# Gate stage of an expert mixer: four PSUM banks for gate matmuls, two for turns, index copies issued by GpSimd, 58 early blocks

## The chip, the cores and the metric

The kernel runs on one core of a Trainium2 chip. A core has five engines, each with its own queue of instructions: TensorE (PE, matmuls), VectorE (DVE), ScalarE (ACT), GpSimd (POOL) and SyncE (SP, which here only issues DMAs). On-chip data lies in SBUF; matmuls write into PSUM, which has eight banks of 128 x 512 32-bit words. The metric is the device time of one launch in microseconds (us), lower is better.

## The reference, cut to what matters

Two layers, each a token mixer (a gated convolution in layer 0, a scan in layer 1) followed by PEER, a mixer over single-neuron experts. The change lies in PEER, which runs for 640 tokens (512 latent, 128 context) of width 1024:

```python
def peer(h, wq, keys, u, v):
    q = (t @ wq).reshape(T, PEER_HEADS, 2, PEER_KEY_DIM // 2)
    s = jnp.einsum('thpe,hpne->thpn', q, keys).astype(jnp.float32)
    s1, i1 = lax.top_k(s[:, :, 0], PEER_TOPK)
    s2, i2 = lax.top_k(s[:, :, 1], PEER_TOPK)
    cand = (s1[..., :, None] + s2[..., None, :]).reshape(T, PEER_HEADS, PEER_TOPK * PEER_TOPK)
    cidx = (i1[..., :, None] * N_KEYS + i2[..., None, :]).reshape(T, PEER_HEADS, PEER_TOPK * PEER_TOPK)
    sc, pos = lax.top_k(cand, PEER_TOPK)
    idx = jnp.take_along_axis(cidx, pos, axis=-1)
    g = jax.nn.softmax(sc, axis=-1).astype(h.dtype)
    ...
        act = jnp.einsum('td,thkd->thk', tb, u[ib])
        return jnp.einsum('thk,thkd->td', jax.nn.gelu(act, approximate=False) * gb, v[ib])
```

There are 128 x 128 = 16384 experts, and each token takes 16 for each of 8 heads, 128 (expert, gate) pairs in all.

## The kernel before, in words

For 464 of the tokens PEER is computed densely: every expert's activation for every token, times a gate that is zero for most. For the other 176 tokens (16, 32 and 128, three groups) the rows of the experts that they chose are gathered from memory.

The experts are cut into 128 blocks of 128. For each there is a U block (activations: 8 pieces of the width, three matmuls each of 128 x 464, since every operand is split into a high and a low part; 24 matmuls into the PSUM tile `pact`, then a gelu by ScalarE into an SBUF tile `ga`, L511) and a V block (`rot` and `acc`, also in threes). A U weight tile of 512 KB is loaded by SP (`ur`, L84), rounded by ScalarE (`uh`, L92), and VectorE takes the rest (`ul`, L101). `mm3` (L128 to L130) issues the three matmuls.

`peer_gates` first computes the queries, top-k lists, expert numbers and gates. Then it copies the expert numbers (`last`) and gates (`SC`) of the first two gathered groups into the columns `cidx` and `cgate`, 24 small DMAs per layer (L935; 8 pairs of 16 x 16 words, 4 pairs of 32 x 32). Then comes the gate stage, which makes the dense gates of the 464 tokens: three times four transposes turn the two parts of the expert numbers and the gates (`gT`, L953, sources I1, I2, SC), each followed by a copy by ScalarE (L956, L958); then 29 chunks of 16 tokens, each with four one-hot tiles by VectorE, four groups of eight matmuls into the PSUM tile `pg` (L999, L1000), each followed by a ScalarE copy into `st` (L1001), and every two chunks a store of `st` to memory (`gdram`). The last four chunks stand in the order of the code; before them a scheduler sets the order of the instructions of each engine.

All through `peer_gates`, `fill` puts in U matmuls to keep PE busy. The U blocks that are done this way (the first `NSP`) are called early blocks; their `ga` is stored to memory by GpSimd (`adram`, L513) and loaded again by SP in the main loop (`load_act`, L570). `ga` has a ring of `LAG + 2` = 5 buffers. The PSUM budget is two banks for `pact`, one for `gT` and three for `pg`.

Then `peer` goes on in the order of the code. It starts two gathers of expert rows (L592) and the load of the first gate tile `gt` (L564) on GpSimd's queue, runs the early blocks that are left but for the last, loads the first three stored blocks, makes `h = ga * gt` for two blocks (L577 on VectorE, rounding `h1` on ScalarE), runs the last early block, and enters the loop over V blocks. An iteration loads and splits a V tile, loads the stored block three ahead (or computes U block a + 3, once the early ones are used up), makes an h, and runs 24 V matmuls: two banks' worth go through `rot`, which VectorE copies or adds into `sacc` (L647, L649). `GATHER` says how many gathered rows are begun per iteration on average while early blocks are used and after.

Of the kernel before, what the change touches and what calls it, by code (L numbers as in the profile page):

```python
# [9 lines left out]
F32 = mybir.dt.float32  # L10
# [11 lines left out]
P = 128  # L22
NL = 512
# [4 lines left out]
G0 = (0, NX[0], sum(NX))  # L28
# [3 lines left out]
HALF = 320  # L32
EPS = 1e-6
NBLK = 128
NSP = 56
LAG = 3
GA = 4
TB = 16
# [1 line left out]
SW = 64  # L40
CH = 5
FILL_Q = (0, 8500)
GATHER = (0.60, 1.98)
START = 4
MORE = (1, 1, 0, 4)
ADA_C = 16
# [70 lines left out]
class K:  # L117
# [28 lines left out]
    def run(s):  # L146
        nc, A = s.nc, s.A
        with ExitStack() as ctx:
# [4 lines left out]
            s.gdram = dram.tile([NBLK // GA, P, ND // SG, GA, SG], F32, name="gdram")  # L153
            s.adram = dram.tile([NSP, P, ND], F32, name="adram")
            s.sdram = dram.tile([1, 2, D], F32, name="sdram")
# [328 lines left out]
    def peer(s, i):  # L484
        nc, A = s.nc, s.A
        with ExitStack() as ctx:
# [15 lines left out]
            def u_blocks():  # L502
                for a in range(NBLK):
# [7 lines left out]
                    nc.scalar.activation(g, pa, AF.Gelu)  # L511
                    if a < NSP:
                        nc.gpsimd.dma_start(s.adram[a], g)  # L513
# [7 lines left out]
            def fill(ns, steps=0):  # L521

                state["owe"] += ns
                while (steps > 0 or ns and state["owe"] > 0) and state["n"] < NSP * KT:
                    t = next(ub)
                    if not steps:
                        state["owe"] -= t
                    steps -= 1 if steps else 0
                    state["n"] += 1
                U.split(state["n"] // KT + 2)  # L530
# [8 lines left out]
            with ExitStack() as mc:  # L539
# [27 lines left out]
                def load_act(a):  # L567
                    if a < NSP:
                        t = ring.tile([P, ND], F32, name="ga")
                        nc.sync.dma_start(t, s.adram[a])  # L570
                        ga[a] = t
# [60 lines left out]
                state["owe"] = 0  # L632
                fill(0, NSP * KT - state["n"] - KT)
                for a in range(LAG):
# [16 lines left out]
                for a in range(NBLK - 2):  # L651
                    V.high(a + 2)
                    if a + LAG >= NSP:
                        U.high(a + LAG + 2)
# [21 lines left out]

                    credit += GATHER[0] if a + LAG < NSP else GATHER[1]
                    due, before = 0, slot
# [72 lines left out]
    def peer_gates(s, i, hi, lo, hrow, cidx, cgate, wq, fill, V, order):  # L751
        nc, A = s.nc, s.A
        with ExitStack() as pc:
# [41 lines left out]
            with qx:  # L795
# [91 lines left out]
                for m in range(16):  # L887

                    o = s.proj_now(wq.get(m), hi, lo, qps, "pq", (lambda: fill(0, 1)) if m == 0 else None, m == 0)
# [31 lines left out]
                def fl(t, n):  # L921
                    return t[:, n].rearrange("p h k -> p (h k)")
# [8 lines left out]
                for g, m in enumerate(NX):  # L931
                    p0 = P - NL + ND + G0[g]
                    for n in range(P // m):
                        for dst, src in ((cidx, last), (cgate, fl(SC, 3))):
                            nc.sync.dma_start(dst[n * m:(n + 1) * m, G0[g]:G0[g] + m], src[p0:p0 + m, n * m:(n + 1) * m])  # L935

            with ExitStack() as gx:
                op = s.pool(gx, "oh", bufs=2)
                sp = s.pool(gx, "stage", bufs=2)
                gps = s.pool(gx, "gps", space=PSUM)  # L940
                tt = s.pool(gx, "tt")

                rep = tt.tile([P, P], F16, name="rep")
                nc.gpsimd.iota(rep, pattern=[[1, P]], base=0, channel_multiplier=0,
                               allow_small_or_imprecise_dtypes=True)
                T1 = tt.tile([P, ND, 2], F16, name="T1")
                T2 = tt.tile([P, ND, 2], F16, name="T2")
                gh = tt.tile([P, ND, 2], F16, name="gh")
                gl = tt.tile([P, ND, 2], F16, name="gl")
                for n, src in ((0, I1), (1, I2), (2, SC)):  # L950
                    o = gps.tile([P, NL], F32, name="gT", bufs=1)
                    for t in range(4):
                        nc.tensor.transpose(o[:, t * P:(t + 1) * P], fl(src, t), s.ident)  # L953
                    twice = o[:, :ND, None].to_broadcast([P, ND, 2])
                    if n < 2:
                        nc.scalar.activation((T1, T2)[n], twice, AF.Copy)  # L956
                    else:
                        nc.scalar.activation(gh, twice, AF.Copy, scale=4096.0)  # L958
                        nc.vector.scalar_tensor_tensor(gl, twice, 4096.0, gh, op0=ALU.mult, op1=ALU.subtract)
                V.prime()  # L960
                TB4 = [P, TB, P // 2, 2]
                OH = {}

                def one_hots(c):
                    sl = slice(c * TB, (c + 1) * TB)
                    pairs = rep.rearrange("p (e b) -> p e b", b=2)[:, None].to_broadcast(TB4)

                    def b(v):
                        return v[:, sl, None, :].to_broadcast(TB4)

                    def new(name, **kw):
                        t = op.tile([P, TB, P], F16, name=name, **kw)
                        return t, t.rearrange("p t (e b) -> p t e b", b=2)

                    _, o2 = new("o2", bufs=1)
                    nc.vector.tensor_tensor(o2, b(T2), pairs, op=ALU.is_equal)
                    o1, o = new("o1")
                    nc.vector.tensor_tensor(o, b(T1), pairs, op=ALU.is_equal)
                    oh, o = new("oh")
                    nc.vector.tensor_tensor(o, b(gh), o2, op=ALU.mult)  # L980
                    ol, o = new("ol")
                    nc.vector.tensor_tensor(o, b(gl), o2, op=ALU.mult)
                    OH[c] = o1, oh, ol

                fill(FILL_T)
                one_hots(0)
                for c in range(ND // TB):
                    if c == ND // TB - G_LAST:
                        order.enter_context(s.tc.manual_schedule())
                    if (c + 1) * TB < ND:  # L990
                        one_hots(c + 1)
                    fill(FILL_G if c < ND // TB - G_LAST else FILL_L)
                    o1, oh, ol = OH.pop(c)
                    if c % 2 == 0:
                        st = sp.tile([P, NBLK // GA, 2, GA, SG], F32, name="st")
                    for t in range(0, TB, 4):
                        g = gps.tile([P, 4, P], F32, name="pg", bufs=3)
                        for q in range(4):
                            nc.tensor.matmul(g[:, q, :], oh[:, t + q, :], o1[:, t + q, :], start=True, stop=False)  # L999
                            nc.tensor.matmul(g[:, q, :], ol[:, t + q, :], o1[:, t + q, :], start=False, stop=True)  # L1000
                        nc.scalar.activation(st[:, :, c % 2, :, t:t + 4], g.rearrange("p t (b a) -> p b a t", a=GA),  # L1001
                                             AF.Copy, scale=1.0 / 4096.0)
                    if c % 2 or c == ND // TB - 1:
                        n = c % 2 + 1
                        nc.scalar.dma_start(
                            s.gdram[:, :, c + 1 - n:c + 1].rearrange("g p c a t -> p g (c a t)"),
                            st[:, :, :n].rearrange("p g c a t -> p g (c a t)"))
# [464 lines left out]
```

## Time and profile before

| | us |
|---|---|
| median of three runs | 4063.26 |
| the three runs | 4061.71, 4071.17, 4063.26 |
| profiled execution | 4057.71 |
| its span in the trace | 4056.0 |
| PE busy | 3915.4 |
| VectorE busy | 3394.0 |
| ScalarE busy | 1663.2 |
| GpSimd busy | 514.9 |

The profiled execution is one more run, with a recording; the numbers of the rows below are of it. Busy times of engines lie beside each other. An engine can be idle because it waits for another; the trace names the releaser. PE's clock can be below full speed ("PEclk" 1.00), and then a busy PE does less.

### The profile page before, as it was taken

The page shows a single profiled execution, that of the slowest core. Times are in us where ns is not written, and L with a number is a line of the kernel's source. Part 1 is how long each engine was busy: PE and PEld are TensorE (multiplying, and loading weights), DVE is VectorE, ACT ScalarE, POOL GpSimd, SP SyncE. Part 2 cuts the span into 40 slices and gives each one's busy share as a digit, 9 for nine tenths or more (in the row PEclk, how much of TensorE's full clock was granted, in tenths as well). Part 3 has the DMA queues.
Part 4 walks back from the last instruction along what each step waited for, and adds up shares of the span by engine and source line. Part 5 has one row for each costly group of instructions (what it writes and reads, how often), then busy time and mean ns, then how long its engine had stood idle before and what let it go on. Part 6 is the DMA issues. An engine that isn't in the chain of part 4 may idle for free.

```text
span 4056.0 us, 59421 instructions
## 1 busy us (share of the span) xinstructions
PE 3915.4 (97%) x22237; PEld 3548.9 (87%) x22237; DVE 3394.0 (84%) x6512; ACT 1663.2 (41%) x3120; POOL 514.9 (13%) x695
## 2 busy tenths in 40 slices
PE   8999999899999999999999999999989999999998
PEld 6989988788888888888899998998878888888887
DVE  8978988588878888887999856998768888888887
ACT  5233344433334333336555644334433333343333
POOL 0010000011112212211110101000011111121211
PEclk9999999999999999999999999999999999999999
DMA  6643258988889989973333234226888898998995
GB/s 228 218 154 121 83 171 248 287 318 312 329 311 338 341 325 333 339 274 126 114 102 119 88 114 173 83 99 192 251 296 314 316 334 316 337 335 329 333 333 222
DMA packets 337451, 979.15 MB, mean 241 GB/s; under 512 B 39371, under 2 KB 174795, under 8 KB 291081
## 3 DMA queue, kind: packets, MB, share of 16 engines
q1 hardware_dynamic: 146922, 508.73, 35.7%
q0 software_dynamic: 64000, 398.47, 26.4%
q10 hardware_dynamic: 126240, 68.16, 5.9%
q8 instruction: 174, 2.85, 0.3%
q14 instruction: 115, 0.94, 0.1%
HBM read 867.00 MB, written 108.14 MB: 240 GB/s over the span
## 4 chain that ended last, share of the span: by engine, by line
issue 41%; PE 29%; DVE 15%; POOL 9%; DMA 4%; ACT 2%; POOLq 0%; SPq 0%; ACTq 0%; DVEq 0%
POOL uv L592 9%; PE pact L128 2%; DMA ur<-uT 2%; PE pact L130 2%; PE pj L128 2%; PE pact L129 2%; PE pj L129 2%; PE pj L130 2%; DVE ul L101 2%; DVE wl L101 1%; PE bank L128 1%; PE bank L129 1%; PE bank L130 1%; PE bank L1189 1%; PE pg L999 1%
## 5 line engine op out<-in xcount | busy, mean ns | idle before, releaser
L128 PE MATMUL pact<-hnh,uh 128*128 128x464 f32 x2048 | 774.2, 378 | 1.0 <-DVE xt L623 1.0
L130 PE MATMUL pact<-hnh,ul 128*128 128x464 f32 x2048 | 768.3, 375 | 0.0
L129 PE MATMUL pact<-hnl,uh 128*128 128x464 f32 x2048 | 766.6, 374 | 0.0
L592 POOL DMA_INDIRECT uv<-uv,cidx x352 | 362.2, 1029 | 1698.6 <-DVE cacc L609 1567.2
L128 PE MATMUL acc<-h,wh 128*128 128x464 f32 x1536 | 575.4, 375 | 0.0
L130 PE MATMUL acc<-h,wl 128*128 128x464 f32 x1536 | 575.3, 375 | 0.0
L129 PE MATMUL acc<-h,wh 128*128 128x464 f32 x1536 | 573.1, 373 | 0.0
L92 ACT ACTIVATE wh<-wr 128x1024 fp32r<-128x1024 f32 x385 | 404.9, 1052 | 377.8 <-DMA wr<-uv 92.5
L599 DVE SCALAR_TENSOR_TENSOR uv<-uv,hrow 128x1024 f32<-128x1024 f32 x352 | 430.1, 1222 | 128.5 <-DMA uv<-uv,cidx 125.3
L101 DVE TENSOR_TENSOR wl<-wr,wh 128x1024 fp32r<-128x1024 f32 x385 | 469.8, 1220 | 54.7 <-ACT wh L92 54.4
L609 DVE SCALAR_TENSOR_TENSOR cacc<-uv,dg,cacc 128x1024 f32<-128x1024 f32 x346 | 443.4, 1282 | 0.0
L130 PEld LDWEIGHTS pact<-hnh,ul 128*128 128x128 f32 x2048 | 386.4, 189 | 45.5 <-DVE ul L101 0.3
L128 PEld LDWEIGHTS pact<-hnh,uh 128*128 128x128 f32 x2048 | 387.2, 189 | 44.6 <-DVE xt L623 1.3
L129 PEld LDWEIGHTS pact<-hnl,uh 128*128 128x128 f32 x2048 | 387.2, 189 | 44.3
L511 ACT ACTIVATE ga<-pact 128x464 f32<-128x464 f32 x256 | 141.8, 554 | 582.6 <-PE pact L130 578.9
L101 DVE TENSOR_TENSOR ul<-ur,uh 128x1024 fp32r<-128x1024 f32 x256 | 312.1, 1220 | 56.0 <-ACT uh L92 55.9
L92 ACT ACTIVATE uh<-ur 128x1024 fp32r<-128x1024 f32 x256 | 268.3, 1050 | 184.7 <-PE pact L129 81.0
L129 PEld LDWEIGHTS acc<-h,wh 128*128 128x128 f32 x1536 | 291.0, 189 | 36.0
L130 PEld LDWEIGHTS acc<-h,wl 128*128 128x128 f32 x1536 | 290.0, 189 | 34.9
L128 PEld LDWEIGHTS acc<-h,wh 128*128 128x128 f32 x1536 | 290.7, 189 | 33.8
L601 ACT ACTIVATE dg<-dg 128x1 f32<-128x1 f32 x352 | 70.6, 200 | 540.4 <-DVE uv L599 540.0
L586 DVE TENSOR_TENSOR h<-h,h 128x464 fp32r<-128x464 f32 x256 | 163.8, 640 | 127.7 <-PE rot L129 123.8
(346 smaller groups left out, 7978.1 us busy)
## 6 DMA issues: line engine op xcount, KB each, us to landing
ur<-uT SPq DMA_DIRECT2D x256, 512.0 KB
wr<-uv SPq DMA_DIRECT2D x256, 512.0 KB
gt<-gdram SPq DMA_DIRECT2D x62, 928.0 KB
gdram<-st ACTq DMA_DIRECT2D x28, 2048.0 KB
mw<-ada_wT SPq DMA_DIRECT2D x80, 512.0 KB
adram<-ga POOLq DMA_DIRECT2D x112, 232.0 KB, 4.1
ga<-adram SPq DMA_DIRECT2D x112, 232.0 KB
wr<-ssd_w SPq DMA_DIRECT2D x48, 512.0 KB
```

Source lines behind the costliest of these rows:

```text
L92: s.K.nc.scalar.activation(hi.rearrange("p a b -> p (a b)"), s.raw[s.nh], AF.Copy)
L101: s.K.nc.vector.tensor_sub(lo.rearrange("p a b -> p (a b)"), s.raw.pop(s.ns), hi.rearrange("p a b -> p (a b)").bitcast(F32))
L128: mm(out, wh, mh, start=start, stop=False)
L129: mm(out, wh, ml, start=False, stop=False)
L130: mm(out, wl, mh, start=False, stop=stop)
L511: nc.scalar.activation(g, pa, AF.Gelu)
L586: nc.vector.tensor_sub(h2, h, h1.bitcast(F32))
L592: nc.gpsimd.indirect_dma_start(out=t[:], out_offset=None, in_=A["uv"].rearrange("l e d -> (l e) d"), in_offset=bass.IndirectOffsetOnAxis(a ...
L599: nc.vector.scalar_tensor_tensor(UV[n][:, :D], UV[n][:, :D], 1.0, rows[-1], op0=ALU.mult, op1=ALU.mult, accum_out=dg[:, n:n + 1])
L601: nc.scalar.activation(dg[:, n:n + 1], dg[:, n:n + 1], AF.Gelu)
L609: nc.vector.scalar_tensor_tensor(cacc, t[:, D:], dg[:, n:n + 1], cacc, op0=ALU.mult, op1=ALU.add)
L999: nc.tensor.matmul(g[:, q, :], oh[:, t + q, :], o1[:, t + q, :], start=True, stop=False)
```

## The change

`NSP` goes from 56 to 58, so two more U blocks of each layer are computed before the loop and reloaded in it. `gT` gets a second PSUM bank and `pg` a fourth, so the gate stage uses all eight banks. The 24 small copies of L935 are issued by GpSimd instead of SP. `GATHER` is a little higher.

```diff
-NSP = 56
+NSP = 58
...
-GATHER = (0.60, 1.98)
+GATHER = (0.62, 2.0)
...
                         for dst, src in ((cidx, last), (cgate, fl(SC, 3))):
-                            nc.sync.dma_start(dst[n * m:(n + 1) * m, G0[g]:G0[g] + m], src[p0:p0 + m, n * m:(n + 1) * m])
+                            nc.gpsimd.dma_start(dst[n * m:(n + 1) * m, G0[g]:G0[g] + m], src[p0:p0 + m, n * m:(n + 1) * m])
...
                 for n, src in ((0, I1), (1, I2), (2, SC)):
-                    o = gps.tile([P, NL], F32, name="gT", bufs=1)
+                    o = gps.tile([P, NL], F32, name="gT", bufs=2)
...
                     for t in range(0, TB, 4):
-                        g = gps.tile([P, 4, P], F32, name="pg", bufs=3)
+                        g = gps.tile([P, 4, P], F32, name="pg", bufs=4)
```

The order of the instructions on PE at the first two turns of layer 0 (`gT` is the bank, `I_2740` and `I_2741` the two sources; `pact` rows are U matmuls), before:

```order
L953 MATMUL gT<-ident,I_2740 128x128 x4
L128 MATMUL pact<-hnh,uh 128x464
L129 MATMUL pact<-hnl,uh 128x464
L130 MATMUL pact<-hnh,ul 128x464
L128 MATMUL pact<-hnh,uh 128x464
L129 MATMUL pact<-hnl,uh 128x464
L953 MATMUL gT<-ident,I_2741 128x128 x4
```

and after, with the third turn (`SC`):

```order
L953 MATMUL gT<-ident,I_2740 128x128 x4
L953 MATMUL gT<-ident,I_2741 128x128 x4
L128 MATMUL pact<-hnh,uh 128x464
L129 MATMUL pact<-hnl,uh 128x464
L130 MATMUL pact<-hnh,ul 128x464
L953 MATMUL gT<-ident,SC 128x128 x4
```

The second turn moved up to the first, and the third now follows three U matmuls later; it reuses the first turn's bank.

On PE in a chunk of the gate stage of layer 0 (difference; `o_6006` is a one-hot tile), before the chunk's fourth group:

```order
 L1000 LDWEIGHTS ol
 L1000 MATMUL pg<-o_6006,ol 128x128
-L128 MATMUL pact<-hnh,uh 128x464
-L129 MATMUL pact<-hnl,uh 128x464
 L999 LDWEIGHTS oh
 L999 MATMUL pg<-o_6006,oh 128x128
```

Two U matmuls that stood ahead of the fourth group are gone from there; they follow behind the group.

On SP at the start of the loop of layer 0, where the first three early blocks are loaded (`ga<-adram`; in brackets the semaphores that each waits for: DMASW are those of DMAs issued by GpSimd, DMAHW of the others), before:

```order
L84 DMA ur_8384<-uT 128x1024 [waits DMAHW5_49,DVE_49]
L570 DMA ga_8418<-adram_64 128x464 [waits DMASW5_49,DMASW4_49,DMASW6_49,DMASW3_49,DMASW7_49,DMASW2_49,DMAHW2_49,DMASW1_49,DMASW0_49]
L570 DMA ga_8420<-adram_64 128x464 [waits DMASW4_49,DMASW6_49,DMASW3_49,DMASW7_49,DMASW1_49,PE_49]
L570 DMA ga_8422<-adram_64 128x464 [waits DMAHW4_49,DMAHW2_49,DVE_49]
L84 DMA ur_8434<-uT 128x1024 [waits DMAHW7_49,Activation_49]
```

and after:

```order
L84 DMA ur_8452<-uT 128x1024 [waits DMAHW1_49,DVE_49]
L570 DMA ga_8486<-adram_64 128x464 [waits DMASW5_49,DMASW6_49,DMASW4_49,DMASW7_49,DMASW3_49,DMAHW4_49,DMASW2_49,DMASW0_49]
L570 DMA ga_8488<-adram_64 128x464 [waits DMASW4_49,DMASW3_49,DMASW6_49,DMASW1_49,DMASW0_49]
L570 DMA ga_8490<-adram_64 128x464 [waits DMAHW6_49,DMASW4_49,DMASW1_49]
L84 DMA ur_8502<-uT 128x1024 [waits DMAHW2_49,DVE_49]
```

The third load no longer waits for VectorE. The counts that the semaphores are compared with stand for these stores: before, the first load waits for the store of block 50 and the second for that of block 51, and the third for VectorE to be done with the first h; after, the three wait for the stores of blocks 52, 53 and 54. On GpSimd's queue the stores of blocks 52 to 54 stand behind the two gathers and the first gate tile, before as after.

## Rows read from the trace of the kernel before

**Rows 1.** The page, busy us, share of the span and instructions of each engine.

```profile
PE 3915.4 (97%) x22237; PEld 3548.9 (87%) x22237; DVE 3394.0 (84%) x6512; ACT 1663.2 (41%) x3120; POOL 514.9 (13%) x695
```

**Rows 2.** PE's waits: what waited <- for what: us in total, times, longest.

```profile
PE rot L128 <- ACT ga L511: 18.2, 2, 9.7
...
PE pg L999 <- ACT st L1001: 14.9, 9, 2.3
...
PE rot L128 <- DVE sacc L647: 6.2, 2, 3.6
...
PE gT L953 <- ACT T L956: 5.5, 2, 2.8
```

**Rows 3.** Windows: stretch, length, busy us (instructions), granted clock, DMA share, GB/s.

```profile
540.00:763.00 223.00, 212.50 (x1660) 185.75 (x1659) 178.60 (x175) 105.94 (x177) 16.18 (x30) 0.98 0.77 234
763.00:787.00 24.00, 15.52 (x78) 13.56 (x75) 5.51 (x6) 6.70 (x10) 4.21 (x6) 0.92 0.92 291
2764.00:2975.00 211.00, 199.96 (x1609) 174.86 (x1608) 167.05 (x148) 103.27 (x174) 15.11 (x28) 0.99 0.79 240
2975.00:3000.00 25.00, 15.29 (x72) 13.37 (x71) 5.52 (x6) 6.34 (x10) 4.49 (x7) 0.90 0.86 278
860.00:900.00 40.00, 40.00 (x192) 35.75 (x192) 33.96 (x48) 14.77 (x26) 4.66 (x5) 1.00 0.88 316
420.00:460.00 40.00, 40.00 (x247) 38.24 (x246) 39.66 (x240) 11.43 (x21) 1.62 (x3) 1.00 0.30 98
```

**Rows 4.** Timeline, PE, loop start of both layers: start, us, instruction, idle before, releaser.

```profile
786.91 0.75 PE L128 MATMUL rot<-h,wh 128*128 128x464 f32 x1 [8.48 <-ACT ga L511]
...
796.54 0.67 PE L128 MATMUL rot<-h,wh 128*128 128x464 f32 x1 [3.61 <-DVE sacc L647]
...
2999.50 0.76 PE L128 MATMUL rot<-h,wh 128*128 128x464 f32 x1 [9.71 <-ACT ga L511]
...
3009.35 0.48 PE L128 MATMUL rot<-h,wh 128*128 128x464 f32 x1 [2.63 <-DVE sacc L647]
```

**Rows 5.** Timelines of GpSimd, VectorE and ScalarE at the loop start of layer 0.

```profile
775.01 1.66 POOL L513 DMA_DIRECT2D adram<-ga  x3
...
784.59 1.19 DVE L577 TENSOR_TENSOR h<-ga,gt 128x464 f32<-128x464 f32 x2 [8.41 <-DMA gt<-gdram]
...
786.32 0.54 ACT L511 ACTIVATE ga<-pact 128x464 f32<-128x464 f32 x1
```

**Rows 6.** DMA queue of GpSimd, 785 to 786 and 2998 to 2999: packets, MB, share.

```profile
q0 software_dynamic: 25, 0.07, 17.6%
...
q0 software_dynamic: 8, 0.02, 5.5%
```

**Rows 7.** The page's DMA issues: stores of early blocks, KB each, us to landing.

```profile
adram<-ga POOLq DMA_DIRECT2D x112, 232.0 KB, 4.1
```

**Rows 8.** The longest wait of a gate matmul (timeline), and the window behind it.

```profile
649.64 0.22 PE L999 MATMUL pg<-o,oh 128*128 128x128 f16 x1 [2.30 <-ACT st L1001]
...
649.60:653.60 4.00, 3.96 (x18) 3.53 (x18) 3.11 (x3) 1.49 (x3) 0.00 (x0) 0.57 0.60 198
```

**Rows 9.** Timelines: a U tile's low part, and the copy that ends the block before.

```profile
703.26 1.22 DVE L101 TENSOR_TENSOR ul<-ur,uh 128x1024 fp32r<-128x1024 f32 x1
...
706.45 0.56 ACT L511 ACTIVATE ga<-pact 128x464 f32<-128x464 f32 x1 [1.23 <-PE pact L130]
```

**Rows 10.** Timelines of ScalarE and PE at the second turn of layer 0.

```profile
555.40 0.93 ACT L956 ACTIVATE T<-gT 128x928 f16<-128x928 f32 x1
...
556.39 0.66 PE L953 MATMUL gT<-ident,I 128*128 128x128 f32 x4 [2.76 <-ACT T L956]
```

**Rows 11.** SP's timeline at the copies of gates; GpSimd's stores by line.

```profile
518.27 4.41 SPq L935 DMA_DIRECT2D cgate<-SC  x7
...
L513 POOL DMA_DIRECT2D adram<-ga x112 | 60.9, 545 | 875.2 <-ACT ga L511 875.2
```

## The prediction

> **What bounds the kernel now.** I read the busy times first: PE works 3915.4 us of the span of 4056.0, VectorE 3394.0 [rows 1], so the end is set by PE, and a change can win only what PE idles or loses in clock, some 140 us. Next PE's waits [rows 2], for those in the code that the change touches: 18.2 us in two waits before the first matmul of the main loop, 14.9 us in nine waits of the gate matmuls (L999) for ScalarE's copies, 5.5 us in two waits at the turns (L953), 6.2 us in two waits on the second bank of the loop. Then the windows [rows 3], to see whether that is all there is: the gate stage (540 to 763) leaves PE 10.5 us idle, in layer 1 11.0, together 21.5, of which the waits of L999 and L953 are 20.4; the boundary behind it (763 to 787, 2975 to 3000) leaves 8.5 and 9.7. In the loop PE has 40.00 us of 40 at full clock. So four places matter, each twice: turns, gate matmuls, boundary, loop.
>
> **The boundary, and two more early blocks.** An early block is 24 matmuls; in the loop 192 matmuls take 40.00 us [rows 3], so 0.208 us each and 5.0 us a block. Two of them leave the loop per layer, where PE is full, so the loop is 10.0 us shorter, and 20.0 for both layers. They go ahead of the loop, where PE idles for 8.48 and 9.71 us [rows 4], so they would be free if the loop's start stood still. It doesn't. In before that start hangs on the gate tile: VectorE begins the first h at 784.59 when it has landed, 8.41 us idle before; two h, two roundings on ScalarE, then the copy of the last early block that is queued behind them and frees the bank, and PE starts at 786.91: 2.3 us in all [rows 4, 5]. The loaded early blocks were no part of it: by the order, the first two loads waited for the stores of blocks 50 and 51, which are out before GpSimd takes up its two gathers and the gate tile. After, load 0 waits for the store of block 52, load 1 for that of 53, load 2 for that of 54, and those stores stand behind gathers and gate tile in GpSimd's queue (in before at 775.01 [rows 5]). That queue's last 0.07 MB pass in 785 to 786, in layer 1 its last 0.02 MB in 2998 to 2999 [rows 6]: say 785.3 and 2998.1. One more U tile (0.524 MB) now goes through ahead; at the 291 GB/s of the boundary [rows 3] that is 1.8 us, which I add in full (bounds 0, if it fits before, and 3.6, if it is twice shared). Then a load of 0.237 MB from issue to landing: no row shows it; 0.8 us at 291 GB/s is the low end, the 4.1 us of a store of the same size [rows 7] the high one; I take 2.9, nearer to the row. So h starts at 790.0 and PE at 785.3 + 1.8 + 2.9 + 2.3 = 792.3, 5.4 later; in layer 1 at 2998.1 + 1.8 + 2.9 + 2.3 = 3005.1, 5.6 later. Of 10.0 us per layer 4.6 and 4.4 remain: 9.0 (with the bounds, 0.8 to 17.1). PE's early blocks end 10.0 later than the 778.43 and 2989.79 of before, so it still idles about 4 and 5 us.
> Right behind it PE waited 3.61 and 2.63 us again, for VectorE's copy of the sum bank [rows 4]; VectorE works on the third h ahead of that copy. Load 2, which feeds it, waited in before for VectorE to be done with the first h, and goes out with the others now, so part of this goes: 3 us with the clock that is low there (0.92 and 0.90 over the boundary [rows 3]); bounds 0 and 8, the clock's whole loss included. Boundary: 12.0 us (0.8 to 25).
>
> **Four banks for the gate matmuls.** A chunk of 16 tokens has four groups; with three banks the fourth waits until ScalarE has emptied the first. ScalarE's copies stand behind its rounding of a U tile, which waits for that tile; so PE stands still although U matmuls are ready behind the group. With a fourth bank PE runs all four groups and goes on with U. Removed: up to 14.9 us in nine waits [rows 2], and a loss of clock behind the longest (2.30 us): 4.0 us at 0.57 [rows 8] cost 1.7. What is late next: the U tile itself. PE arrives at it up to 2.3 us earlier. In the tightest place that I found, VectorE's low part of a tile ends at 704.48, and PE is done with the block before at 706.45 [rows 9]: 2.0 us of slack. I take 12.5 of the 16.6 (bounds 0 and 16.6; below nothing is excluded, since no matmul is added and PE keeps its order otherwise).
>
> **Two banks for the turns.** By the order the second turn now follows the first at once, and the third has to wait for ScalarE's copy out of the first, the same copy that the second waited for. That copy starts at 555.40 and takes 0.93 us, and PE stood 2.76 us until 556.39 for it [rows 10]; the third turn has fewer U matmuls ahead (three for five, 0.4 us), but the wait for the second copy behind it, had there been one, goes as well. Cost and gain: 0 (bounds a gain of 1 and a loss of 1).
>
> **Copies of indices and gates by GpSimd.** 24 per layer, of 1 KB and 4 KB. On SP they held the queue for 4.41 us (seven of them [rows 11]) while U tiles are loaded ahead of need; there I expect nothing. On GpSimd a direct DMA takes 545 ns in the mean, over all 112 stores [rows 11], so twelve take 6.5 us. What is queued behind them is the store of the next early block, which frees a buffer of a ring of five; PE waits only when five blocks, 25 us, have gone by, so from 2.1 us per copy. I take 0.
> A page of the Trainium skill, "SBUF — State Buffer", section "Summary: rules for kernel authors", speaks against it: DMAs should not be issued by GpSimd, since VectorE's fast modes lock it out of the port it writes descriptors through; it gives some 3.1 us for an issue beside such copies. By that estimate twelve would take 37 us, 12 past the ring's 25, and the sum would be about 24 us worse, 4063. Against it stands the 0.545 us here: between 420 and 460 VectorE was busy 39.66 of 40 us and GpSimd's three instructions took 1.62 us together [rows 3].
>
> **GATHER.** The gathers are issued a little sooner and more evenly; by the order, one iteration issued three of them before and none issues more than two after, and the first two changes of the token group move by one iteration. PE has 40.00 of 40 us and DMA a share of 0.88 there [rows 3], with VectorE at 33.96. 0; were DMA the limit, the two blocks' U tiles less per layer would rather help, and the denser gathers cost up to 9.
>
> **Sum.** 12.0 + 12.5 = 24.5 us less than the profiled 4057.71 (span 4056.0 and 1.7 around it): 4033.2. The median of the runs is 4063.26, 5.55 above the profiled execution; so 4038.7, say 4039.
>
> **Rivals.**
> A. All the waits named go, the turn's too: 16.6 + 5.5 + 20.0 + 6.2 = 48 us, 4015. For it: the loads' latency has no row. Against it: by the order the loads wait behind stores, and the third turn for the same copy.
> B. The gate waits come back as waits for U tiles, since both hang on one late transfer: 12.0 remain, 4051. For it: slack of 2.0 us at the tightest block, and waits of up to 2.3. Against it: eight more of the nine are shorter, 1.6 on average.
> C. The boundary only moves: the loop starts 10 us later, since stores and loads take turns with the U tiles on the same engines (DMA share 0.92 there [rows 3]); 12.5 remain, 4051.
> D. Slower: GpSimd takes the copies one after another, each as long as a transfer that it has to see landed, 4.1 us [rows 7]. Twelve copies of the gates are 49 us, 24 past the ring; those of the indices stand behind two stores, 8 and 4, so they cost from 3.2 us each, 11 more; 35 per layer, 70 less 24.5: 4108. It makes the kernel slower than before from 3.2 us per copy. Against it are 112 stores of 545 ns [rows 11], and no row shows a small one that took longer.
> E. No gain from another side: the loop loses up to 9 us by the gathers' spread: 4048, or with B or C about 4060.
>
> **How the numbers follow.** What a measurement of this kernel can tell from no change is 0.3%, 12.2 us: faster is below 4051.1. The forecast (4026 to 4050) has 0.52, A 0.08, B 0.15, C 0.15, D 0.05, E 0.05. B and C lie on the bound, half of each counts as faster: 0.52 less 0.01, 0.08 and 0.15 make 0.74. Same: the other half, E and that 0.01, so 0.20 with 0.01 of D; slower the rest, 0.06 with a part of E. The range leaves out D, the lower half of A, and the ends of the others: 4019 to 4057.
>
> **What the changed profile would show.** PE's wait of L999 on ScalarE's copies gone or below 3 us, and no more than 3 us of new waits of U matmuls on VectorE (else B). The turn's wait still there, two of about 2.8 us, now at SC. PE idle ahead of the loop 3 to 6 us instead of 8.48 and 9.71, with the first h waiting for a reloaded block and no longer for the gate tile; if it is still the gate tile, A is nearer; if PE idles 8 us or more, C. The wait for the sum bank at 1 to 2 us. GpSimd's copies at 0.5 to 0.6 us each; above 2.1 us, D. In the loop PE 40.00 of 40, else E.

## The result and the profile after

The changed kernel takes 4024.16 us in the median of three runs (4022.69, 4024.16, 4027.67), before 4063.26; the ratio is 0.9900 (95% interval 0.9879 to 0.992), 33 to 49 us less. The forecast was 4039, with a range of 4019 to 4057: direction and range held, but the gain was 39 us where 24.5 were forecast, and the time lies below the forecast's own 4026 to 4050. The profiled execution took 4027.67 (span 4025.9), 30 less than the profiled execution of before, which was on the fast side of its kernel: over the later runs of the kernel before, times went from 4050 to 4079 with medians of 4061 to 4064. So a difference of two profiled executions can be off by some 10 us, and the parts below go by medians of runs on one chip. Two later runs, of 5598.71 and 7791.52 us, were in a slower state and are left out of the medians.

The page's busy times, after, which answer to [rows 1]: PE has as much work as before in a shorter span.

```profile
span 4025.9 us, 59465 instructions
...
PE 3915.7 (97%) x22237; PEld 3555.7 (88%) x22237; DVE 3398.8 (84%) x6512; ACT 1663.5 (41%) x3120; POOL 545.5 (14%) x747
```

PE's waits, after, against [rows 2] (what waited <- for what: total, times, longest):

```profile
PE rot L128 <- DVE sacc L649: 11.7, 9, 2.5
PE rot L128 <- ACT ga L511: 10.4, 2, 6.2
...
PE gT L953 <- ACT T L956: 5.6, 2, 2.9
...
PE rot L128 <- DVE sacc L647: 4.5, 2, 3.4
...
PE pact L622 <- DVE cacc L609: 2.8, 2, 2.4
```

The wait of L999, 14.9 us, has no row any more, and no row of U matmuls on `ul` or `uh` came in its place. The wait ahead of the loop went from 18.2 to 10.4. The turns wait as before. The windows of the gate stage and of the boundary up to the loop's start, after (columns as in [rows 3]):

```profile
540.00:757.00 217.00, 214.05 (x1689) 190.91 (x1688) 185.10 (x187) 107.73 (x181) 22.67 (x43) 0.99 0.79 242
757.00:786.00 29.00, 24.86 (x119) 21.91 (x117) 7.96 (x8) 8.91 (x13) 5.32 (x8) 0.98 0.96 314
2750.00:2957.00 207.00, 204.40 (x1642) 182.32 (x1641) 174.29 (x162) 105.81 (x178) 21.61 (x41) 0.99 0.82 250
2957.00:2987.00 30.00, 23.78 (x112) 20.96 (x112) 7.66 (x8) 7.73 (x11) 6.06 (x9) 0.93 0.89 289
```

In the gate stage PE idles 3.0 and 2.6 us instead of 10.5 and 11.0: little more than the turns' waits. In the boundary it idles 4.1 and 6.2, at a granted clock of 0.98 and 0.93 for 0.92 and 0.90. The start of layer 0's loop, after, on GpSimd, SP, VectorE, ScalarE and PE, and PE in layer 1, against [rows 4, 5]:

```profile
769.29 1.68 POOL L513 DMA_DIRECT2D adram<-ga  x3
...
780.62 1.41 SPq L570 DMA_DIRECT2D ga<-adram  x3
...
783.54 1.20 DVE L577 TENSOR_TENSOR h<-ga,gt 128x464 f32<-128x464 f32 x2 [2.18 <-DMA ga<-adram]
...
785.26 0.54 ACT L511 ACTIVATE ga<-pact 128x464 f32<-128x464 f32 x1
...
785.86 0.76 PE L128 MATMUL rot<-h,wh 128*128 128x464 f32 x1 [4.14 <-ACT ga L511]
...
2986.51 0.76 PE L128 MATMUL rot<-h,wh 128*128 128x464 f32 x1 [6.22 <-ACT ga L511]
```

The first h now waits for a reloaded block and no longer for the gate tile, as the prediction had it: from load to h 783.54 - 780.62 = 2.9 us. From the three stores to the loop's first matmul it takes 785.86 - 769.29 = 16.6 us, against 786.91 - 775.01 = 11.9 in [rows 4, 5]: 4.7 later, where 5.4 were worked out. In layer 1 it takes 17.1 against 11.9, 5.2 later for 5.6.

### The profile page after: what moved, and what is told of

It is laid out like the page before. It is cut to its first block, busy times and chain, and to the rows that moved or that the text cites. A ratio compares the mean times of both kernels' runs of the same rounds, so it can differ in the third digit from the quotient of the medians.

```text
span 4025.9 us, 59465 instructions
## 1 busy us (share of the span) xinstructions
PE 3915.7 (97%) x22237; PEld 3555.7 (88%) x22237; DVE 3398.8 (84%) x6512; ACT 1663.5 (41%) x3120; POOL 545.5 (14%) x747
## 4 chain that ended last, share of the span: by engine, by line
issue 40%; PE 33%; DVE 13%; POOL 9%; DMA 3%; ACT 2%; POOLq 0%; SPq 0%; ACTq 0%; DVEq 0%
POOL uv L592 9%; PE pact L128 3%; PE pact L130 3%; PE pact L129 3%; PE pj L128 2%; PE pj L129 2%; PE pj L130 2%; PE pg L999 1%; PE pg L1000 1%; DVE wl L101 1%; DVE ul L101 1%; DMA uv<-uv,cidx 1%; PE bank L128 1%; PE bank L129 1%; PE bank L130 1%
```

## The experiments

All runs are of five rounds, against the kernel before on the same chip; "us less" is the difference of the medians, the interval that of the ratio in us.

**One part at a time.** The fourth bank for the gate matmuls alone:

```diff
-                        g = gps.tile([P, 4, P], F32, name="pg", bufs=3)
+                        g = gps.tile([P, 4, P], F32, name="pg", bufs=4)
```

> The kernel before with the fourth bank for the gate matmuls alone. My prediction's term: 12.5 us less, because some of the gate waits come back as waits for U tiles. Second theory, from the trace after: nothing comes back, the whole 14.9 us of waits and the 1.7 us of clock go, and the gathers and the gate tile start that much earlier too: 16 to 18 us less. Rival B of the prediction: the waits return as waits for U tiles, under 4 us less. In the profile PE's wait of L999 for L1001 is gone under all three; the waits of pact for ul tell B apart.

4042.7 against 4063.64: 20.9 less (14.6 to 28.0). The waits didn't come back as U waits; rival B falls. The prediction's 12.5 lies outside the interval. PE's waits at the loop's start, and the rows of L999 by line (instructions | busy, mean ns | idle before) in this kernel:

```profile
PE rot L128 <- ACT ga L511: 24.7, 2, 12.5
```

```profile
L999 PE MATMUL pg<-o,oh 128*128 128x128 f16 x928 | 110.8, 220 | 0.0
```

and that row in the kernel before:

```profile
L999 PE MATMUL pg<-o,oh 128*128 128x128 f16 x928 | 115.7, 220 | 15.2 <-ACT st L1001 14.9
```

The wait is gone, and more with it. From the first turn to the loop's first matmul both kernels do the same work; the windows of both layers (columns as in [rows 3]) in the kernel before, and then with the fourth bank:

```profile
551.97:786.91 234.94, 215.96 (x1677) 188.67 (x1675) 172.22 (x154) 109.63 (x183) 19.32 (x34) 0.98 0.80 244
2764.36:2999.50 235.14, 214.39 (x1677) 187.47 (x1675) 172.21 (x154) 109.61 (x183) 19.34 (x34) 0.98 0.80 244
```

```profile
555.66:781.23 225.57, 210.40 (x1676) 187.33 (x1674) 173.55 (x154) 109.04 (x183) 19.31 (x34) 0.98 0.82 254
2763.50:2988.85 225.35, 210.41 (x1676) 187.33 (x1674) 173.59 (x154) 108.96 (x183) 19.99 (x34) 0.98 0.82 255
```

That is 9.4 and 9.8 us less, 19.2 in all: PE idles 9.6 less and is busy 9.5 less. The granted clock up to the end of the gate matmuls is 1.00 in both layers, for 0.98 and 0.99 before. How much of the 9.5 is clock isn't separated; my term had 1.7. Over the whole span PE's busy time is not less in this execution (3917.6 for 3915.4), since stages that the edit doesn't touch ran at a lower clock (0.97 for 0.98 ahead of the first turn), so its profile alone shows only 10 us. With early blocks done sooner, 6.5 us more are waited ahead of the loop (24.7 for 18.2), which two more early blocks can then use.

Two more early blocks alone:

```diff
-NSP = 56
+NSP = 58
```

> The kernel before with 58 early blocks alone. My prediction: 12 us less (20 us out of the loop, the loop's start 5.5 us later in each layer, 3 us of the second stall); PE idles 4 to 5 us ahead of the loop in each layer and the first h waits for a reloaded block. Rival C: the loop's start moves by the full 10 us, within 2 us of before. Second theory, from the trace after, where layer 1's loop was 16.8 us shorter and layer 0's 8.4: two blocks are worth more in the loop than their 10 us per layer, 14 to 18 us less.

4073.69 against 4063.64: 10.1 more (7.3 to 16.7), against all theories. The boundary did what was forecast (its wait fell from 18.2 to 8.7 us), but a wait came at the loop's end. PE's waits, and PE at the end of layer 0's loop:

```profile
PE rot L128 <- ACT wh L92: 21.4, 2, 11.9
...
PE rot L128 <- ACT ga L511: 8.7, 2, 4.5
```

```profile
1811.94 0.75 PE L128 MATMUL rot<-h,wh 128*128 128x464 f32 x1 [11.88 <-ACT wh L92]
```

VectorE shows why: in the last iteration it waits for one gathered row after another.

```profile
1805.88 1.22 DVE L599 SCALAR_TENSOR_TENSOR uv<-uv,hrow 128x1024 f32<-128x1024 f32 x1 [5.06 <-DMA uv<-uv,cidx]
...
1809.14 1.23 DVE L599 SCALAR_TENSOR_TENSOR uv<-uv,hrow 128x1024 f32<-128x1024 f32 x1 [0.83 <-DMA uv<-uv,cidx]
```

The code's own count says the same. With 58 blocks, 55 iterations at 0.60 and 71 at 1.98 give 173.6 of 176 gathers, and the loop does all that are left, five, in its last iteration; before it was 53 x 0.60 + 73 x 1.98 = 176.3, two there.

The second bank for the turns alone (`gT`, bufs=2), and the copies by GpSimd alone (L935):

> The kernel before with the second bank for the turns alone. My prediction: 0 (within 1 us), the wait of L953 stays at 2 x 2.8 us. Rival A: the waits go, 5 to 8 us less.

> The kernel before with the 24 index and gate copies per layer issued by GpSimd alone. My prediction: 0 (within 3 us), each copy 0.5 to 0.6 us on GpSimd. Rival D: 4.1 us each, about 70 us more in all; by the 3.1 us of the Trainium skill's page "SBUF — State Buffer" about 24 us more. Another rival: U tiles are no longer held up on SP, some us less.

Turns: 4065.77, 2.1 more (5.7 less to 5.7 more), the wait still there, 5.3 us in two. Copies: 4059.35, 4.3 less (8.5 less to 0.8 more), no loss. GpSimd's copies by line in this kernel (columns as for L999):

```profile
L935 POOL DMA_DIRECT2D cgate<-SC x24 | 11.8, 501 | 9.9 <-DVE SC L918 9.9
L935 POOL DMA_DIRECT2D cidx<-last x24 | 11.7, 494 | 5.9 <-DVE last L930 5.9
```

0.5 us each: rival D falls.

**The pair, the rate alone, and the whole.**

```diff
-NSP = 56
+NSP = 58
-GATHER = (0.60, 1.98)
+GATHER = (0.62, 2.0)
```

> The kernel before with 58 early blocks and the higher gather rate, nothing else. Theory: 58 early blocks alone left three gathers for the last loop iteration, and PE stood 2 x 10.7 us for them; with the rate raised along, the 12 us of my prediction come out, or with the loop of layer 1 up to 20. Rival: the two blocks bring nothing by themselves and need the earlier end of the gate stage (the fourth bank): within 4 us of before.

> The kernel before with the higher gather rate alone. My prediction: 0. Second theory: the scattered waits of the loop (16 us for the sum banks, and the clock behind them) come from its uneven gathers, and are fewer with the new rate: 5 to 8 us less. Third: it brings on gathers at a place where DMA is full, up to 9 us more.

> The changed kernel once more, to have it beside the others on the same chip: 39 us less than before by the medians of the first runs, 30 by the two profiled executions; between these.

Against 4064.27: the pair 4042.55, 21.7 less (11.4 to 24.4); the rate alone 4053.8, 10.5 less (5.7 to 15.9); the whole 4020.36, 43.9 less (35.4 to 49.2). So with the new rate the two blocks are worth 21.7 - 10.5 = 11.2, where 12.0 were forecast (by the ratios, 0.9956 for the pair and 0.9973 for the rate, it is 6.9, so this difference is known to some us only), and with the old one they cost 10.1: the difference, 21.3, is as large as the 21.4 us of waits in the loops' last iterations. The parts add up to about the whole: 20.9 + 10.5 + 11.2 + 4.3 - 2.1 = 44.8.

**Why does the rate alone gain 10 us?** The traces, one of each kernel, have it in the loops. PE waits less often until VectorE has added the bank `rot` into its sum (L649), with the new rate alone 5.5 us against 15.8 in eleven waits before:

```profile
PE rot L128 <- DVE sacc L649: 5.5, 2, 3.7
```

and the two loops, in the kernel before and with the new rate alone:

```profile
786.91:1830.80 1043.89, 1029.81 (x4862) 916.58 (x4862) 872.05 (x1129) 389.80 (x758) 182.25 (x180) 0.99 0.87 320
2999.50:4038.99 1039.49, 1025.25 (x4862) 911.71 (x4863) 869.23 (x1128) 387.84 (x755) 179.17 (x175) 0.99 0.87 320
```

```profile
794.48:1826.89 1032.41, 1023.09 (x4862) 912.59 (x4862) 873.37 (x1129) 390.00 (x758) 182.53 (x180) 0.99 0.88 324
3000.78:4038.19 1037.41, 1026.16 (x4862) 915.07 (x4863) 871.96 (x1128) 387.53 (x755) 179.92 (x175) 0.99 0.88 321
```

Together they are 13.6 us shorter. In the three runs above that leave the loop as it was (the gate banks, the turns and the copies alone) these waits are 14.5 to 18.4 us, and the loops are within 3 us of before. It is no full account, for in the changed kernel, which has the same rate, the waits are 11.7 again. What the rate changes in the loops is less clear. With the old rate one iteration (a = 62) has three gathers, since the one before is cut to one at the change of the token group, and the change to the second group falls in iteration 26, where a gate tile is loaded too. With the new rate no iteration has three, the change falls in 25, and the last iteration has no gather left, where it had two. The first two were taken away, each by itself, on the kernel before: at most two gathers per iteration, and the gate tile one iteration later.

```diff
-                    while slot + due < NG and (credit >= 1 or a == NBLK - 3) and not (due and slot + due in G0):
+                    while slot + due < NG and (credit >= 1 or a == NBLK - 3) and not (due and slot + due in G0) and due < 2:
```

> The kernel before, old gather rate, with at most two gathers per iteration. Theory: the rate matters because it leaves one iteration with three gathers (a = 62, right after the change of the token group), where VectorE's add into the sum bank stands behind them and PE waits 1.2 to 2.5 us with a loss of clock behind; without it 4 to 8 us less than before, and the wait some 390 us into the loop is gone in both layers. Rival: the rate's gain comes from the place of the changes of the token group or from an earlier end of the gathers: within 3 us of before.

```diff
-                    if a % GA == GA - 2:
+                    if a % GA == GA - 1:
                         load_g(a // GA + 2)
```

> The kernel before, old gather rate, with the load of a gate tile one iteration later in every four (a mod 4 = 3 instead of 2). Theory: with the old rate the change to the second token group falls in iteration 26, where a gate tile is loaded too, and the two gathers of that place, the row tile, the gate tile and the reloaded blocks collide: h waits 2 to 5 us for a reloaded block and PE 2.2 to 4.0 us some 155 us into the loop, with a loss of clock behind; with the new rate it falls in iteration 25. So this kernel loses that wait in both layers, and the wait some 390 us in: 5 to 10 us less than before. Rival: it is not the gate tile but the pair of gathers there, and the wait stays: within 3 us of before.

4061.64 against 4062.87 (8.5 less to 2.4 more), and 4060.98 against 4060.77 (5.7 less to 2.8 more). VectorE's waits between 920 and 960 show that the second edit took its wait away; the kernel before, and then the edited one:

```profile
DVE h L577 <- DMA ga<-adram: 3.5, 1, 3.5
DVE xt L623 <- PE pact L622: 2.1, 1, 2.1
```

```profile
DVE h L586 <- PE rot L129: 5.6, 4, 1.9
DVE xt L623 <- PE pact L622: 2.0, 1, 2.0
```

and PE's wait some 155 us into the loop (2.2 us in layer 1 before) is gone with it, as it is with the new rate; with at most two gathers the wait some 390 us in (2.5 and 1.2 before) is gone. But the waits for the sum bank are still 15.5 us in all with at most two gathers, and 10.9 with the later gate tile, and neither kernel is measurably faster. So two single waits are explained, the 10.5 us are not: it may be both together, or the end of the gathers; that wasn't tried.

**The start of the loop.** Stores from block 50 on by ScalarE, on the changed kernel:

```diff
-                        nc.gpsimd.dma_start(s.adram[a], g)
+                        (nc.scalar if a >= 50 else nc.gpsimd).dma_start(s.adram[a], g)
```

> The changed kernel with the stores of the early blocks from block 50 on issued by ScalarE instead of GpSimd, so that they don't stand behind the two gathers and the gate tile. My reading of the loop's start (the first load waits for the store of block 52 behind gathers and gate tile): the first h waits for the gate tile again, or for nothing, PE's wait of 4.1 and 6.2 us ahead of the loop falls below 2 us each, 8 to 14 us less than the changed kernel. Rival: gathers, gate tile, stores and U tiles share the DMA engines, so the order of issue changes nothing: within 3 us of it.

4022.4, 2.0 more than the whole in the same set: no gain. The wait ahead of the loop did fall, to 2.1 us in all, but ScalarE stood still. Its timeline (stores in its queue):

```profile
757.59 0.37 ACTq L1005 DMA_DIRECT2D gdram<-st  x1
758.03 5.13 ACTq L513 DMA_DIRECT2D adram<-ga  x1
763.26 1.06 ACT L92 ACTIVATE uh<-ur 128x1024 fp32r<-128x1024 f32 x1 [5.26 <-issue]
```

The store right behind the 2 MB store of gates took 5.13 us to issue, and the rounding of a U tile waited behind it; PE's waits for `uh`, `ul` and `st` rose by some 11 us.

GpSimd's queue in another order instead, with the stores of blocks 52 and 53 first, then the gate tile, then the gathers:

```diff
-                gather(0)
-                gather(1)
-                load_g(0)
...
                 state["owe"] = 0
+                fill(0, 54 * KT - state["n"])
+                load_g(0)
+                gather(0)
+                gather(1)
```

> The changed kernel with GpSimd's queue at the loop's start in another order: the stores of blocks 52 and 53 ahead of the gate tile and the two gathers, the gate tile ahead of the gathers. Theory: the first load then waits for nothing late and the gate tile lands sooner, PE's waits of 4 and 6 us ahead of the loop go; 8 to 14 us less than the changed kernel. Rival, after the run with stores by ScalarE: what is won there comes back in the first iterations, since the same bytes pass the same DMA engines: within 4 us of it.

4012.97 against 4062.87: 49.9 less than before (44.7 to 59.3), beside 43.9 (35.4 to 49.2) of the changed kernel; 6 to 7 us more gain in the medians, on another chip and in intervals that overlap. The wait ahead of the loop fell to 6.4 from 10.4, and the second behind it rose in layer 1:

```profile
PE rot L128 <- DVE sacc L647: 6.5, 2, 5.2
PE rot L128 <- ACT ga L511: 6.4, 2, 4.6
```

The two waits together are only 2.0 us less than in the changed kernel (12.9 for 14.9), so it isn't shown where the rest of those 6 to 7 us would come from. Last, two more early blocks with a rate that leaves none over (58 to 60, rate 0.67 and 2.0):

> The changed kernel with 60 early blocks and a gather rate of 0.67 and 2.0 (no iteration with three, none left over). By the boundary step of my prediction two more blocks per layer move the loop's start by some 5 of their 10 us until PE's idle time ahead of it is used up, 4 to 6 us of which are left: 8 to 12 us less than the changed kernel. Rival C: the loop's start moves by the whole 10 us: within 3 us of it.

4015.74: 47.1 less than before (43.9 to 58.5), 3 to 5 more than the whole, less than the 8 to 12 that the boundary step gave; whether it is more than nothing, as rival C has it, these intervals don't tell. The wait ahead of the loop is used up: 1.4 us in the two layers together. Either kernel's median is below the changed kernel's; the first has the lowest of all that were run, but the two are not told apart.

## Why the prediction was right or wrong

**Boundary, two early blocks: right, on a condition that it missed.** 12.0 forecast, 11.2 measured, known to some us. The chain (load behind stores, h behind load, PE behind h) is in the trace with 4.7 and 5.2 us for 5.4 and 5.6. The wait right behind the loop's start gave 1.7 us, where the term had 3 with the clock: 6.2 us before, 4.5 after (1.1 and 3.4, where 1 to 2 each were forecast). Its bounds were added up wrongly: the parts it names give 3.0 to 16.8 us ahead of that wait, for the 0.8 to 17.1 stated. But the term holds only because the gather rate was raised with the block count; alone the blocks cost 10.1.

**Four gate banks: right mechanism, too small.** 12.5 forecast, bound 16.6, measured 20.9 (14.6 to 28.0). I held back 4 us for U tiles that would be late; none were. And of the 9.5 us that PE was busy less in this stage the sum had only the 1.7 us of clock behind the longest wait; on the other side it lacked the 6.5 us that come back as a wait ahead of the loop.

**GATHER: wrong.** "0; were DMA the limit..." was the step: by itself it gained 10.5 (5.7 to 15.9), and it kept the block count from losing 21. I read the loop from one window with PE at 40.00 of 40, while over the whole loops of before PE idles 14.1 and 14.2 us: the window had none of the uneven places, the changes of the token group and the last iteration. In the view of PE's waits before, from which I took four rows, this one stood between them, and I left it out:

```profile
PE rot L128 <- DVE sacc L649: 15.8, 11, 3.9
```

With the new rate alone 5.5 us of it are left; by what in the order of the gathers is open. With 8.4 us on the banks and 10.5 here the miss of some 19 us against the whole's 43.9 is made up, in medians that are each good to some us.

**Turns and copies: right.** Neither part, run by itself, is told apart from the kernel before. The third turn waits where the second did. After, in layer 0:

```profile
556.92 1.03 PE L953 MATMUL gT<-ident,I 128*128 128x128 f32 x8
561.54 0.66 PE L953 MATMUL gT<-ident,SC 128*128 128x128 f32 x4 [2.95 <-ACT T L956]
```

The copies take 0.5 us as the stores did. The Trainium skill's page "SBUF — State Buffer", section "A bandwidth-pool intuition that's wrong (but worth ruling out)", gives about 3.1 us for a DMA issued by GpSimd that overlaps a copy by VectorE. That did not show: by the prediction's estimate it would have made 24 us more, and 4.3 less were measured. It isn't refuted either, since beside them VectorE ran no copy longer than 0.32 us in the run of the copies alone.

## What to carry to other kernels

Read a loop at its uneven places (a group change, the last iteration), not in a window from its middle, and count what a rate leaves over when the number of iterations changes: here a rate that came out 2.4 gathers short cost 21 us. A wait that goes with a buffer can take more than its own row with it, and part of it comes back at the next meeting point, so edits that use the freed time belong in the same trial. Where a transfer waits behind others of its queue, moving it to another engine's queue can stop that engine.

## What was not expected of the hardware

Six stores of 232 KB that ScalarE issued as the first DMA behind one of its 2 MB stores, 0.4 to 2.8 us after that store's issue began, took 3.07 to 5.55 us to issue, while the ten others took 0.33 or 0.34: issuing stopped the engine. The copies of 1 and 4 KB that GpSimd issued took 0.49 to 0.51 us each in the mean, no longer than its stores of 232 KB (548 ns).
